# Channel mixer, hidden pairs f = 3 to 9: two plain products replaced by Strassen's seven, with weight sums made by GpSimd

## The chip, the core and the metric

The kernel runs on one core of one Trainium2 chip. The metric is the device time of one execution in microseconds (us); lower is better. Engines are named as in the profile: PE is TensorE (matmuls), PEld its weight loads, DVE is VectorE, ACT is ScalarE, POOL is GpSimd, SP is SyncE. SPq and POOLq are the DMA issues of SP and POOL. Each engine takes its instructions strictly in the order of its own list; that list is fixed when the kernel is built.

## The reference, cut to what matters

One layer: two token mixers, then a SwiGLU channel mixer with 22 hidden blocks of 128 channels, then a norm.

```python
h2 = rmsnorm(x, norm2_w[l])                                   # 512 tokens x 1024
f_gate, f_up = jnp.split(h2 @ ffn_w_gate_up[l], 2, axis=-1)   # 2816 + 2816 columns
x = x + (jax.nn.silu(f_gate) * f_up) @ ffn_w_down[l]
return rmsnorm(x, norm_f_w)
```

Each fp32 product is made of three matmuls: both factors are split into a rounded part ("hi") and the rest ("lo"), and hi·hi, hi·lo and lo·hi are added.

## The kernel before, in words

The change lies in the first half of the channel mixer, from about 618 to 843 us of the profiled execution. A **pair** f (0 to 21) is hidden block f of the gate (`wgu[f]`) and of the up projection (`wgu[FF + f]`), over all 512 tokens.

**Plain pairs, f < F0 = 10** (lines 1076 to 1098). `col_tile` calls `unit`, which loads a 128x1024 weight tile `raw` by SP, lets ACT write `whi` (L111) and DVE the rest `wlo` (L112), and issues 24 matmuls of 512 columns (8 blocks of the inner dimension, three terms each). A pair is two such tiles: 48 matmuls. ACT makes the silu `cw` (L1086), DVE the product `fm`. The pairs f = 0 and 1 are partly done ahead, in `norm2`.

**Strassen pairs, f >= F0** (`pair`, from L1109). The gate and up tiles, each cut in two halves of the inner dimension, are the blocks A11, A12, A21, A22 of a 2x2 matrix; the activations are cut in four likewise. Seven products of 12 matmuls each, 256 columns wide, take the place of the 48 wide ones: 84 matmuls. They need four weight units, in this order: `w` = (A11, A12), `w46` = (A22, s2), `w37` = (s4, s3), `w5` = (s1), with s1 = A21 + A22, s2 = A11 + s1, s3 = A11 + A21, s4 = A12 + s2. These sums are read from DRAM.

**Who makes the sums.** `feed_one` (L186) has SP copy one block within DRAM and then has POOL issue a DMA that adds the other block to it (L196). This goes on from the first stage of the kernel to about 736 us, one sum per weight unit. An s2 waits for its s1, an s4 for its s2.

**The sums for the down projection.** `dsums_to(f)` does, for odd f and while any are left, one round of this: POOL issues a load of a 1 MB tile `wst` (L166), adds blocks in it by four 128x512 additions (L172), and issues the store to `wsum` (L173). The pool of `wst` has one buffer, so that the next load waits until the store has left it. Four rounds are left for this stage.

**The activations' sums** `xb0` to `xb3` and their splits T1 to T4 (`th`, `tl`) are made by DVE and ACT from a list `todo`, one entry per weight tile, spread over the plain pairs. `some_operands(f)` makes the operands `fh`, `fl` of the down projection from the finished `fm`, from f = 7 on.

**Buffers and order.** `raw`, `whi` and `wlo` have three buffers each: ACT can write the `whi` of a unit when PE has finished the unit three places before. The order in which each engine gets its instructions is not that of the code: a scheduler at build time places them by dependences, priorities and its own estimates. So an instruction written late can stand early in its engine's list.

Of the kernel before, what the change touches and what calls it, by code (L numbers as in the profile page):

```python
# [14 lines left out]
P = 128  # L15
T = 512
# [4 lines left out]
FF = 22  # L21
# [11 lines left out]
def block_kernel(ctx, tc, a):  # L33
    nc = tc.nc
    V, S, G, PE = nc.vector, nc.scalar, nc.gpsimd, nc.tensor
# [3 lines left out]
    wp = ctx.enter_context(tc.tile_pool(name="wp", bufs=3))  # L39
# [57 lines left out]
    loads, start_feed, gps_ = [], [False], []  # L97
# [3 lines left out]
    def unit(ap, pool=None):  # L101

        aps = ap if isinstance(ap, tuple) else (ap,)
        n = T * len(aps) if isinstance(ap, tuple) else 1024
        raw, hi, lo = ((pool or wp).tile([P, n if pool else 1024], t, name=x)[:, 0:n]
                       for t, x in ((F32, "raw"), (F32R, "whi"), (F32R, "wlo")))
        for i, p in enumerate(aps):
            loads.append(nc.sync.dma_start(raw[:, i * T:(i + 1) * T] if len(aps) > 1 else raw, p))
        if start_feed[0]:
            fill()  # L110
        marked(S.activation(hi, raw, AF.Copy), "unit")  # L111
        marked(V.tensor_tensor(out=lo, in0=raw, in1=hi.bitcast(F32), op=ALU.subtract), "unit")  # L112
        return hi, lo
# [31 lines left out]

    FK, F0 = FF // 2, 10
    sums = {n: dram.tile([FF - F0, P, T], F32, name=n, bufs=1) for n in ("s1", "s2", "s3", "s4")}
    gu = {n: a["wgu"][r * FF + F0:(r + 1) * FF][:, :, c * T:(c + 1) * T]  # L150
          for n, r, c in (("A11", 0, 0), ("A12", 0, 1), ("A21", 1, 0), ("A22", 1, 1))}
# [13 lines left out]
    def dsums_load(k, r, eng, cs=slice(0, T)):  # L165
        eng.dma_start(r, a["wdn"][k].rearrange("p (i c) -> p i c", i=4)[:, :, cs])  # L166
# [33 lines left out]
    def fill():  # L200

        units[0] += 1
        if units[0] % 3 != 2 or not gps_:
            feed_one()
        if taken and units[0] % 3 != 2 and not norming[0]:
            dsums_add(*taken.pop(0))
        if halves and gps_ and units[0] > 3 and not taken and not norming[0] and (units[0] % 2 == 0 if len(gps_) == 1 else units[0] % 3 == 0):
            half_load()
# [3 lines left out]
    with tc.tile_pool(name="st", bufs=2) as st:  # L212
# [56 lines left out]
        for k in range(KD):  # L269
            w = vec[:, k:k + 1]  # L270
# [3 lines left out]
            if k % 2 == 0:  # L274
                c = slice(k * P, k * P + 256)
# [24 lines left out]
        raw, hi, lo = early[3]  # L300
# [41 lines left out]
        for k in range(2, 4):  # L342
# [6 lines left out]
                        in1=ss[:, 1].rearrange("p (n a) -> p n a", a=1).broadcast_to([P, NT, 16]), op=ALU.mult)  # L349
# [6 lines left out]
                        in1=rowp[:, 1:2, :].broadcast_to([P, NT, H]), op=ALU.add)  # L356
# [9 lines left out]
        with tc.issue_after(ln_.ins):  # L366
            for g_ in gated:
# [8 lines left out]
                        op=ALU.mult)  # L376
# [445 lines left out]
    while step() or chains:  # L822
# [4 lines left out]
        for c in list(chains):  # L827
            if c[0] <= count[0] or not queue:
                with behind():
                    n = next(c[1], None)  # L830
# [160 lines left out]
    fxs = ctx.enter_context(ExitStack())  # L991
# [9 lines left out]
    def tt(out, in0, in1, op, eng=V):  # L1001
        return eng.tensor_tensor(out=out, in0=in0, in1=in1, op=op)  # L1002
# [5 lines left out]
    def hidden():  # L1008
        fms.append(fp.tile([P, T], F32, name="fm"))
        return fms[-1]  # L1010
# [17 lines left out]
    def dsums_to(f):  # L1028
        if f % 2 and rest:
            k, cs = rest.pop(0)  # L1030
            if rest and rest[0][0] == k:
                rest.pop(0)
                cs = slice(0, T)
            r = fs.tile([P, 4, T], F32, name="wst")[:, :, 0:cs.stop - cs.start]
            dsums_load(k, r, nc.gpsimd, cs)
            dsums_add(k, r, cs)
# [25 lines left out]
    def some_operands(f):  # L1062
        if not ff:
            fxs.close()
            ff.append(ctx.enter_context(tc.tile_pool(name="ff", bufs=FK)))
        for _ in range(3 if f < F0 else 2):
            if len(made) <= f:
                operands(len(made))
                made.append(1)

    def next_todo():
        if todo:
            with behind():
                todo.pop(0)()

    for f in range(F0):
        start_feed[0] = f > 0
        dsums_to(f)
        if f > 1:
            pg = psm.tile([P, T], F32, name="mm")  # L1080
            col_tile(pg, a["wgu"][f], hhk, hlk)
        else:
            pg = first[2 * f][0]
            k_loop(*first[2 * f], slice(2 * P, T))
        sg = fq.tile([P, T], F32, name="cw", bufs=2)
        S.activation(sg, pg, AF.Silu)  # L1086
        if f:
            next_todo()
            pu = psm.tile([P, T], F32, name="mm")
            col_tile(pu, a["wgu"][FF + f], hhk, hlk)  # L1090
        else:
            pu = first[1][0]
            k_loop(*first[1], slice(2 * P, T))
        tt(hidden(), pu, sg, ALU.mult)
        if f:
            next_todo()
        if f > 6:
            some_operands(f)

    def hprod(ps, w, i, x):  # L1100

# [7 lines left out]
    def pair(f):  # L1109

        z = [bank() for _ in range(4)] if f % 2 == 0 else [bank(), bank2(), bank2(), bank2()]
        s = lambda n: sums[n][f - F0]
        w = unit(a["wgu"][f])
        w46 = unit((a["wgu"][FF + f][:, T:], s("s2")))
        hprod(z[0][:, t1], w, 0, B11)
        hprod(z[1][:, t1], w, 1, B21)
        hprod(z[2][:, t1], w46, 0, T4)
        w37 = unit((s("s4"), s("s3")))
        hprod(z[0][:, t2], w46, 1, T2)
        cw = fq.tile([P, T], F32, name="cw", bufs=2)  # L1120
        S.copy(out=cw[:, t1], in_=z[0][:, t1])
        u = fq.tile([P, TH], F32, name="cu")
        tt(u, cw[:, t1], z[0][:, t2], ALU.add)
        hprod(z[1][:, t2], w37, 0, B22)
        w5 = unit((s("s1"),))
        hprod(z[3][:, t1], w37, 1, T3)
        v = fq.tile([P, TH], F32, name="cv2")
        tt(v, u, z[3][:, t1], ALU.add)
        if f == F0:
            xsplit(*T1, b11)  # L1130
        hprod(z[2][:, t2], w5, 0, T1)
        tt(cw[:, t2], u, z[2][:, t2], ALU.add)
        fm = hidden()
        tt(fm.rearrange("p (i t) -> p i t", i=2), z[2].rearrange("p (i t) -> p i t", i=2),
           v.rearrange("p (a t) -> p a t", a=1).broadcast_to([P, 2, TH]), ALU.add)
        tt(cw, cw, z[1], ALU.add)
        S.activation(cw, cw, AF.Silu)
        V.scalar_tensor_tensor(out=fm, in0=fm, scalar=-1.0, in1=cw, op0=ALU.mult, op1=ALU.mult)

    for f in range(F0, FF):  # L1140
        pair(f)
        dsums_to(f)
        some_operands(f)


    fqs.close()
# [220 lines left out]
```

## Time and profile before

| | us |
|---|---|
| median of 3 runs (lowest to highest) | 957.11 (956.86 to 957.43) |
| the profiled execution | 957.3 |
| its span | 955.5 |
| outside the span | 1.8 |
| first matmul of f = 2 | 634.29 |
| first matmul of f = 10 (first Strassen pair) | 721.33 |
| first matmul of the down projection | 842.82 |
| POOL busy, whole span | 350.4 |

Views used: the page's busy times and its chain; the waits of an engine in a stretch of time; the timeline of one engine, where a row is start, busy time, engine, line, operation, output<-inputs, how many such instructions in a row (then the busy time is that of all), and in brackets the idle time before it and what ended it. PE rows overlap, since matmuls are pipelined: their pace is read from start to start, not from the busy time.

### The profile page before, as it was taken

Reading aid. Unit: us, or ns where it says so; the run is one execution under the profiler, and the core shown is the slowest. Engines: PE = TensorE matmul, PEld = TensorE weight load, DVE = VectorE, ACT = ScalarE, POOL = GpSimd, SP = SyncE. Lnnn points to the kernel's source line nnn. Section 1 sums busy time; section 2 is a strip of 40 time slices with the busy share of each in tenths; the row PEclk is TensorE's granted clock in tenths of the full one; section 3 lists DMA queues with packets and bytes.
Section 4 is the critical chain, followed back from the end, with each engine's and each line's share of the span. In section 5 each row is a group of like instructions: output and inputs, shape, how many; then the busy total and the mean of one; then the engine's idle time right before and its main releaser. Section 6 shows DMA issues by size and latency. Waiting matters only on the chain.

```text
span 955.5 us, 14889 instructions
## 1 busy us (share of the span) xinstructions
PE 942.1 (99%) x5208; PEld 794.2 (83%) x5208; DVE 729.6 (76%) x1134; ACT 535.3 (56%) x1102; POOL 350.4 (37%) x555
## 2 busy tenths in 40 slices
PE   9999999999999999999999999999999999999997
PEld 6778888887887888888877888888889999988885
DVE  4999887876888888898877753766425887888896
ACT  7697786969756674634546323323324445456545
POOL 1136434344533447444163432254351111133042
PEclk9999999999999999999999999999999999999999
DMA  9234322233232246979887984598899655578654
GB/s 324 104 128 118 102 82 86 92 99 101 70 92 87 89 133 158 316 223 267 273 274 220 315 235 172 181 264 290 277 255 216 198 188 190 177 228 262 210 178 155
DMA packets 78186, 177.39 MB, mean 186 GB/s; under 512 B 10080, under 2 KB 19472, under 8 KB 77088
## 3 DMA queue, kind: packets, MB, share of 16 engines
q1 hardware_dynamic: 66528, 144.89, 45.5%
q0 software_dynamic: 10288, 28.90, 13.4%
q10 hardware_dynamic: 1296, 2.67, 0.7%
q8 instruction: 41, 0.67, 0.3%
q14 instruction: 33, 0.27, 0.1%
HBM read 156.22 MB, written 45.37 MB: 211 GB/s over the span
## 4 chain that ended last, share of the span: by engine, by line
PE 85%; ACT 3%; DVE 3%; issue 2%; DMA 1%; POOL 1%; POOLq 0%; SPq 0%; ACTq 0%; DVEq 0%
PE mm L121 57%; PE w L121 19%; PE g L437 1%; DMA raw<-s 1%; DVE wlo L112 1%; PE st L616 1%; PE st L610 1%; PE b L542 1%; PE g L470 1%; PE b L548 1%; PE b L566 1%; PE st L604 1%; PE g L519 1%; PE st L615 1%; PE st L605 1%
## 5 line engine op out<-in xcount | busy, mean ns | idle before, releaser
L111 ACT ACTIVATE whi<-raw 128x1024 fp32r<-128x1024 f32 (+1 forms) x191 | 196.2, 1029 | 240.7 <-PE mm L121 143.6
L112 DVE TENSOR_TENSOR wlo<-raw,whi 128x1024 fp32r<-128x1024 f32 (+1 forms) x191 | 240.5, 1260 | 88.0 <-ACT whi L111 87.4
L121 PE MATMUL mm<-hh,whi 128*128 128x512 f32 (+1 forms) x688 | 268.9, 391 | 0.3 <-ACT hh L336 0.3
L121 PE MATMUL mm<-hl,whi 128*128 128x512 f32 (+1 forms) x688 | 264.4, 384 | 0.0
L121 PE MATMUL mm<-hh,wlo 128*128 128x512 f32 (+1 forms) x688 | 263.6, 384 | 0.2 <-DVE wlo L112 0.2
L672 DVE SCALAR_TENSOR_TENSOR cps<-c,c31w,cps 128x512 f32<-128x512 f32 x240 | 180.3, 751 | 6.1 <-ACT cps L670 1.8
L121 PEld LDWEIGHTS mm<-hh,wlo 128*128 128x128 f32 x688 | 129.6, 188 | 23.6 <-DVE wlo L112 0.4
L121 PEld LDWEIGHTS mm<-hh,whi 128*128 128x128 f32 x688 | 129.7, 189 | 22.5 <-ACT hh L336 0.8
L121 PEld LDWEIGHTS mm<-hl,whi 128*128 128x128 f32 x688 | 129.9, 189 | 20.8
L1002 POOL TENSOR_TENSOR fm<-fm 128x256 f32<-128x256 f32 x33 | 28.0, 850 | 111.9 <-DVE s L1002 87.4
L424 DVE SCALAR_TENSOR_TENSOR acc<-mm,c4w,acc 128x511 f32<-128x511 f32 (+2 forms) x72 | 53.1, 741 | 6.1 <-ACT acc L421 5.9
L506 POOL TENSOR_TENSOR ytm<-U,y 128x60 f32<-128x60 f32 (+14 forms) x120 | 37.1, 309 | 48.2 <-DMA U<-sc 39.4
L121 PE MATMUL mm<-yl,whi 128*128 128x512 f32 x128 | 50.0, 391 | 2.3 <-DVE yl L861 2.3
L121 PE MATMUL mm<-yh,whi 128*128 128x512 f32 x128 | 50.7, 396 | 0.0
L121 PE MATMUL mm<-yh,wlo 128*128 128x512 f32 x128 | 49.9, 390 | 0.0
L121 PE MATMUL w<-hh,wlo 128*128 128x256 f32 x168 | 47.7, 284 | 0.3 <-DVE wlo L112 0.3
L121 PE MATMUL w<-hh,whi 128*128 128x256 f32 x168 | 47.6, 284 | 0.0
L121 PE MATMUL w<-hl,whi 128*128 128x256 f32 x168 | 47.5, 283 | 0.0
L121 PE MATMUL w<-wlo,fh 128*128 128x512 f32 (+1 forms) x115 | 44.3, 385 | 0.2 <-DVE wlo L112 0.2
L121 PE MATMUL w<-whi,fh 128*128 128x512 f32 (+1 forms) x115 | 44.2, 385 | 0.0
L121 PE MATMUL w<-whi,fl 128*128 128x512 f32 (+1 forms) x115 | 44.2, 384 | 0.0
L196 POOL DMA_DIRECT2D s<-in_wgu_dram x24 | 23.6, 997 | 47.9 <-DMA s<-in_wgu_dram 47.9
(332 smaller groups left out, 1915.8 us busy)
## 6 DMA issues: line engine op xcount, KB each, us to landing
raw<-in_win_dram SPq DMA_DIRECT2D x61, 512.0 KB, 3.5
raw<-in_wgu_dram SPq DMA_DIRECT2D x32, 512.0 KB, 3.6
s<-in_wgu_dram SPq DMA_DIRECT2D x48, 256.0 KB, 5.3
raw<-s SPq DMA_DIRECT2D x48, 256.0 KB, 3.6
raw<-wsum SPq DMA_DIRECT2D x44, 256.0 KB, 3.8
raw<-in_wdn_dram SPq DMA_DIRECT2D x33, 256.0 KB, 3.5
s<-in_wgu_dram POOLq DMA_DIRECT2D x24, 256.0 KB, 7.2
s<-s POOLq DMA_DIRECT2D x24, 256.0 KB, 7.0
```

The costliest lines, as they stand in the source:

```text
L111: marked(S.activation(hi, raw, AF.Copy), "unit")
L112: marked(V.tensor_tensor(out=lo, in0=raw, in1=hi.bitcast(F32), op=ALU.subtract), "unit")
L121: marked(PE.matmul(ps, l, r, start=first and i == 0, stop=last and i == 2))
L196: fed.append(nc.gpsimd.dma_start(*begun.pop(0), accum_op=ALU.add, max_dma_last_dim=2048))
L424: marked(V.scalar_tensor_tensor(out=acc[:, s:], in0=ps[:, :T - s], scalar=c4w[:, j, k:k + 1], in1=acc[:, s:], op0=ALU.mult, op1=ALU.add))
L437: PE.transpose(ps[:, n, :], src[:, n, :], ident)
L470: PE.matmul(ps[:, n, :], kT[:, n, :], kT[:, n, :], start=True, stop=True)
L506: G.tensor_tensor(out=tm[:, :, 0:w], in0=U[:, k, :, k + 1:], in1=y[:, :, k:k + 1].broadcast_to([P, NT, w]), op=ALU.mult)
L519: PE.matmul(ps[:, n, :], kT[:, n, :], qT[:, n, :], start=True, stop=True)
L542: PE.matmul(ps[:, n, 0:16], Ud[:, n, :], xc[:, n, 0:16], start=True, stop=True)
L672: V.scalar_tensor_tensor(out=acc, in0=c[:, k:k + T], scalar=c31w[:, i, k:k + 1], in1=acc, op0=ALU.mult, op1=ALU.add)
L1002: return eng.tensor_tensor(out=out, in0=in0, in1=in1, op=op)
```

## The change

Pairs f = 3 to 9 go through `pair` too (FS = 3). Their weight sums are not taken from DRAM. `summed(f)` loads the gate and the up tile of pair f into one tile `z` of seven 128x512 blocks (two buffers) and has POOL add four times within it: s3 = A11 + A21, then s1 in the place of A21, then s2, then s4. It is called for f = 3 during f = 0, and otherwise at the start of the pair before. `halves_of` takes the place of `unit` and splits blocks of `z`: no `raw` tile is loaded.

The loop of plain pairs is left with f = 0, 1, 2. Their `next_todo` takes three entries at a time instead of one. `dsums_to` and `some_operands` are called from f = 10 on only; `some_operands` then makes up to two operands a call.

```diff
-    FK, F0 = FF // 2, 10
+    FK, FS, F0 = FF // 2, 3, 10
...
-        for _ in range(3 if f < F0 else 2):
+        for _ in range(2):
...
+    fz = fxs.enter_context(tc.tile_pool(name="fz", bufs=2))
+    zs = {}
+    def summed(f):
+        z = zs[f] = fz.tile([P, 7, T], F32, name="z")
+        for i, r in ((0, f), (2, FF + f)):
+            loads.append(nc.sync.dma_start(z[:, i:i + 2].rearrange("p i c -> p (i c)"), a["wgu"][r]))
+        a11, a12, a21, a22, s2, s4, s3 = (z[:, i] for i in range(7))
+        for o, x, y in ((s3, a11, a21), (a21, a21, a22), (s2, a11, a21), (s4, a12, s2)):
+            tt(o, x, y, ALU.add, G)
+    def halves_of(z, i, n=2):
+        hi, lo = (wp.tile([P, 1024], F32R, name=x)[:, 0:n * T] for x in ("whi", "wlo"))
+        if start_feed[0] and i in (0, 5):
+            fill()
+        src = z[:, i:i + n].rearrange("p i c -> p (i c)")
+        marked(S.activation(hi, src, AF.Copy), "unit")
+        marked(V.tensor_tensor(out=lo, in0=src, in1=hi.bitcast(F32), op=ALU.subtract), "unit")
+        return hi, lo
...
-    for f in range(F0):
+    for f in range(FS):
         start_feed[0] = f > 0
-        dsums_to(f)
...
-        if f > 6:
-            some_operands(f)
+        else:
+            summed(FS)
...
-        w = unit(a["wgu"][f])
-        w46 = unit((a["wgu"][FF + f][:, T:], s("s2")))
+        if f + 1 < F0:
+            summed(f + 1)
+        w = halves_of(zs[f], 0) if f < F0 else unit(a["wgu"][f])
+        w46 = halves_of(zs[f], 3) if f < F0 else unit((a["wgu"][FF + f][:, T:], s("s2")))
...
-    for f in range(F0, FF):
+    for f in range(FS, FF):
         pair(f)
-        dsums_to(f)
-        some_operands(f)
+        if f >= F0:
+            dsums_to(f)
+            some_operands(f)
```

**POOL's list.** Before the change, in the plain pairs, the rounds of `wst` (one number for each round) alternate with the issues of the feed (L196):

```order
L172 TENSOR_TENSOR wst_6452<-wst_6452 128x512 x4
L173 DMA wsum_136<-wst_6452 128x2048
L196 DMA s3_127<-in_wgu_dram 128x512
L166 DMA wst_6594<-in_wdn_dram 128x2048
L196 DMA s2_126<-s1_125 128x512
L196 DMA s1_125<-in_wgu_dram 128x512
L172 TENSOR_TENSOR wst_6594<-wst_6594 128x512 x4
```

After the change, from the last addition but one for f = 4 (tile `z_6611`) to the third for f = 5 (tile `z_6740`):

```order
L1002 TENSOR_TENSOR z_6611<-z_6611 128x512
L166 DMA wst_8043<-in_wdn_dram 128x2048
L1002 TENSOR_TENSOR z_6611<-z_6611 128x512
L172 TENSOR_TENSOR wst_8043<-wst_8043 128x512 x4
L173 DMA wsum_137<-wst_8043 128x2048
L166 DMA wst_8318<-in_wdn_dram 128x2048
L172 TENSOR_TENSOR wst_8318<-wst_8318 128x512 x4
L173 DMA wsum_138<-wst_8318 128x2048
L1002 TENSOR_TENSOR z_6740<-z_6740 128x512
L196 DMA s1_125<-in_wgu_dram 128x512
L1002 TENSOR_TENSOR z_6740<-z_6740 128x512
L196 DMA s4_128<-s2_126 128x512
```

All four rounds of `wst`, called from f = 11 on in the code, stand among the additions for f = 3 to 6; two whole rounds stand between those for f = 4 and those for f = 5. Right behind, the last round stands around the first additions for f = 6 (tile `z_6867`):

```order
L1002 TENSOR_TENSOR z_6740<-z_6740 128x512
L166 DMA wst_8599<-in_wdn_dram 128x2048
L1002 TENSOR_TENSOR z_6740<-z_6740 128x512
L172 TENSOR_TENSOR wst_8599<-wst_8599 128x512 x3
L1002 TENSOR_TENSOR z_6867<-z_6867 128x512
L172 TENSOR_TENSOR wst_8599<-wst_8599 128x512
L1002 TENSOR_TENSOR z_6867<-z_6867 128x512
L196 DMA s3_127<-in_wgu_dram 128x512
L1002 TENSOR_TENSOR z_6867<-z_6867 128x512
```

The third addition of each `z` is s2, which `w46` needs; the first round (`wst_7768`) is mixed likewise with the four additions for f = 3 (`z_6455`). For f = 7 to 9 no round is left among them.

**DVE's list.** DVE now has the activations' sums and splits close together, ahead of the first `wlo` taken from `z`; before, each stood between two weight tiles. After the change, from the `wlo` of the gate of f = 2:

```order
L112 TENSOR_TENSOR wlo_6532<-raw_6530,whi_6531 128x1024
L1002 TENSOR_TENSOR xb2_6392<-xb2_6392,xb0_6390 128x1024
L1002 TENSOR_TENSOR xb3_6393<-hh_92,hl_93 128x1024
L112 TENSOR_TENSOR wlo_6571<-raw_6569,whi_6570 128x1024
L1002 TENSOR_TENSOR xb3_6393<-xb2_6392,xb3_6393 128x1024
L1051 SCALAR_TENSOR_TENSOR tl0_6395<-xb2_6392,th0_6394 128x1024
L1002 TENSOR_TENSOR fm_6524<-mm_6491,cw_6486 128x512
L999 TENSOR_TENSOR tl2_6399<-xb3_6393,th2_6398 128x1024
L999 TENSOR_TENSOR tl1_6397<-xb1_6391,th1_6396 128x1024
L1090 TENSOR_TENSOR wlo_6619<-z_6455,whi_6618 128x1024
```

The work on the activations that stood between the weight tiles of f = 1 to 9 now stands before the first product of f = 3.

More of the change, by code (lines that the diff above doesn't have):

```diff
@@ L1069, in some_operands @@
                 made.append(1)
-    def next_todo():
-        if todo:
-            with behind():
-                todo.pop(0)()
-    for f in range(F0):
+    fz = fxs.enter_context(tc.tile_pool(name="fz", bufs=2))
[15 more added lines that the diff above has]
+        return hi, lo
+    def next_todo():
+        for _ in range(3):
+            if todo:
+                with behind():
+                    todo.pop(0)()
+    for f in range(FS):
         start_feed[0] = f > 0
-        dsums_to(f)
         if f > 1:
@@ L1117, in pair @@
         hprod(z[2][:, t1], w46, 0, T4)
-        w37 = unit((s("s4"), s("s3")))
+        w37 = halves_of(zs[f], 5) if f < F0 else unit((s("s4"), s("s3")))
         hprod(z[0][:, t2], w46, 1, T2)
@@ L1124, in pair @@
         hprod(z[1][:, t2], w37, 0, B22)
-        w5 = unit((s("s1"),))
+        w5 = halves_of(zs[f], 2, 1) if f < F0 else unit((s("s1"),))
         hprod(z[3][:, t1], w37, 1, T3)
@@ L1128, in pair @@
         tt(v, u, z[3][:, t1], ALU.add)
-        if f == F0:
+        if f == FS:
             xsplit(*T1, b11)
```

## The prediction

> **What bounds the kernel now.** First the page's busy times and its chain, then what PE waited for between 600 and 845 us (a row is engine, line, waited for, total, times, longest).
>
> ```profile
> span 955.5 us, 14889 instructions
> PE 942.1 (99%) x5208; PEld 794.2 (83%) x5208; DVE 729.6 (76%) x1134; ACT 535.3 (56%) x1102; POOL 350.4 (37%) x555
> PE 85%; ACT 3%; DVE 3%; issue 2%; DMA 1%; POOL 1%; POOLq 0%; SPq 0%; ACTq 0%; DVEq 0%
> PE w L121 <- DVE wlo L112: 0.3, 1, 0.3
> PE mm L121 <- DVE wlo L112: 0.2, 1, 0.2
> ```
>
> PE is busy for 99% of the span, carries 85% of the chain, and in the stage of the change waits 0.5 us in all. The number of matmuls times their pace sets the time here, so fewer columns help; and any wait that PE gets is added to the end in full. The pace comes from three first matmuls on PE's timeline:
>
> ```profile
> 634.29 0.39 PE L121 MATMUL mm<-hh,whi 128*128 128x512 f32 x1
> 721.33 0.28 PE L121 MATMUL w<-hh,whi 128*128 128x256 f32 x1
> 842.82 0.40 PE L121 MATMUL w<-whi,fh 128*128 128x512 f32 x1
> ```
>
> They begin f = 2, f = 10 and the down projection. Eight plain pairs take 721.33 - 634.29 = 87.04 us, 10.88 each; twelve Strassen pairs 121.49 us, 10.12 each, or 0.1205 for each of 84 matmuls.
>
> **What the change removes.** Seven pairs at 10.88 - 10.12 = 0.76 us: **5.3 us off PE**, if it never waits. All else is whether the operands come in time.
>
> **What it adds.** POOL gets 28 additions of 128x512. The same shape stands in the rounds of `wst` (L172); POOL's timeline has all four rounds:
>
> ```profile
> 618.17 0.87 POOL L166 DMA_DIRECT2D wst<-in_wdn_dram  x1
> 625.29 0.81 POOL L196 DMA_DIRECT2D s<-s  x1 [5.12 <-DMA s<-s]
> 627.68 8.55 POOL L172 TENSOR_TENSOR wst<-wst 128x512 f32<-128x512 f32 x4 [1.58 <-DMA wst<-in_wdn_dram]
> 636.53 0.60 POOL L173 DMA_DIRECT2D wsum<-wst  x1 [0.30 <-POOL wst L172]
> 642.86 0.57 POOL L166 DMA_DIRECT2D wst<-in_wdn_dram  x1 [4.86 <-issue]
> 651.11 7.13 POOL L172 TENSOR_TENSOR wst<-wst 128x512 f32<-128x512 f32 x4 [5.97 <-DMA wst<-in_wdn_dram]
> 658.54 0.59 POOL L173 DMA_DIRECT2D wsum<-wst  x1 [0.30 <-POOL wst L172]
> 664.02 0.57 POOL L166 DMA_DIRECT2D wst<-in_wdn_dram  x1 [4.02 <-DMA wsum<-wst]
> 664.58 0.89 POOL L196 DMA_DIRECT2D s<-in_wgu_dram  x1
> 674.13 5.78 POOL L172 TENSOR_TENSOR wst<-wst 128x512 f32<-128x512 f32 x4 [8.67 <-DMA wst<-in_wdn_dram]
> 680.22 0.59 POOL L173 DMA_DIRECT2D wsum<-wst  x1 [0.31 <-POOL wst L172]
> 685.71 0.56 POOL L166 DMA_DIRECT2D wst<-in_wdn_dram  x1 [4.03 <-DMA wsum<-wst]
> 693.90 6.46 POOL L172 TENSOR_TENSOR wst<-wst 128x512 f32<-128x512 f32 x4 [6.75 <-DMA wst<-in_wdn_dram]
> ```
>
> Read from it: an addition costs 1.44 us (5.78 / 4) to 2.14 (8.55 / 4), 1.75 in the mean of the four (6.98 / 4). From the issue of a load to the first addition pass 9.5, 8.3, 10.1 and 8.2 us, 9.0 in the mean. From the issue of a store to the next load 6.3, 5.5 and 5.5, mean 5.8. An issue takes 0.6 (wst) or about 0.85 (feed). Before, a wait on POOL delayed only other sums needed far later.
>
> Why 8.55 in one round and 5.78 in another is seen on DVE's timeline:
>
> ```profile
> 627.16 1.22 DVE L112 TENSOR_TENSOR wlo<-raw,whi 128x1024 fp32r<-128x1024 f32 x1
> 628.29 2.32 DVE L1002 TENSOR_TENSOR xb<-xb,xb 128x1024 f32<-128x1024 f32 x1
> 630.54 2.31 DVE L112 TENSOR_TENSOR wlo<-raw,whi 128x1024 fp32r<-128x1024 f32 x1
> 635.00 0.68 DVE L1002 TENSOR_TENSOR fm<-mm,cw 128x512 f32<-128x512 f32 x1
> 637.24 1.21 DVE L1002 TENSOR_TENSOR xb<-xb,xb 128x1024 f32<-128x1024 f32 x1
> ```
>
> POOL adds from 627.68 to 636.23. Well inside, a DVE operation with both inputs in SBUF takes 2.32 (2.25 from start to start); after it 1.21. One that reads PSUM (`mm`) takes its usual 0.68. So the two engines slow each other: 2.14 on POOL and 2.25 on DVE while both work in SBUF.
>
> **The step that decides** is POOL's list. Two whole rounds of `wst` stand between the last addition for f = 4 and the first for f = 5, and one load of `wst` before the first for f = 6. POOL takes its list in order: at 674.13 it had stood idle for 8.67 us for its load. Step by step, with 0.3 from an addition's end to the store:
>
> - Round 1 and f = 3: eight additions from 627.68 at 2.14 (DVE works throughout: ten operations of 2.25 wait for it), an s4 issue and a store: 627.68 + 17.1 + 0.8 + 0.6 = 646.2.
> - f = 4: three additions and two feed issues ahead of the load of round 2: + 6.4 + 1.7 = 654.3.
> - Round 2: + 9.0 to the first addition, + 7.0 for four, + 0.3 + 5.8 to the next load: 676.4.
> - Round 3: + 9.0, + 5.8 for four (DVE stands by then), + 0.9 for the store: 692.1.
> - f = 5: three additions at 1.44 and two feed issues: + 6.0 = 698.1. Then ACT's `whi`, 1.06 in the row below, and DVE's `wlo`, 1.2: PE can go on at **700.4**.
>
> ```profile
> 639.70 1.06 ACT L111 ACTIVATE whi<-raw 128x1024 fp32r<-128x1024 f32 x1 [4.38 <-PE mm L121]
> ```
>
> PE would want this `wlo` in f = 5's third product: 634.29 + 10.88 + 2 x 10.12 + 24 x 0.1205 + 0.24 = 668.5. **It waits 31.9 us.** Nothing on ACT or DVE can pass: the `whi` and `wlo` that wait are ahead of all that is for later pairs.
>
> - f = 6: the load of round 4 is issued behind the third addition, at 698.1; + 9.0, then seven additions to this pair's s2 (three of `wst`, `z`, `wst`, `z`, `z`) at 1.6, between alone and contended since DVE is half idle, and one feed issue: 719.2; + 2.3 = **721.5**. PE wants it at 700.1 + 60 x 0.1205 + 2.89 + 0.24 = 710.5: **11.0 more.**
> - The rest of f = 6 is 60 matmuls: 721.2 + 7.2 = 728.5. Then the clock:
>
> ```profile
> 1.00 4.02 PE L258 MATMUL g<-one 128*128 128x512 bf16 x9 [1.00 <-DVE epsc L73]
> 7.10 0.39 PE L121 MATMUL mm<-ul,whi 128*128 128x512 f32 x1
> 7.33 0.40 PE L121 MATMUL mm<-uh,whi 128*128 128x512 f32 x1
> 948.00:950.00 2.00, 0.36 (x4) 0.16 (x2) 1.55 (x7) 0.18 (x2) 0.17 (x1) 1.00 0.68 262
> 952.00:954.00 2.00, 0.00 (x0) 0.00 (x0) 0.00 (x0) 0.00 (x0) 0.00 (x0) 0.59 0.59 229
> 954.00:955.50 1.50, 0.00 (x0) 0.00 (x0) 0.00 (x0) 0.00 (x0) 0.00 (x0) 0.50 0.00 0
> ```
>
> At the start nine matmuls take 0.45 each, and a start-to-start of 0.23 comes only from 7.10: about 5.9 us at half pace. At the end (stretches; PE busy first, granted clock last but two) PE stops at 948.4 and the clock is halved by about 952.4. Waits of 32 and 11 us halve it too. The first slow stretch lies in front of a wait for POOL and costs nothing; the second costs at most 5.9 / 2 = 2.9, nothing at least; I take 2.9: 731.4. The Trainium skill's page "TensorE: Matmul & The Clock Gate" (Part 1, What's actually happening) puts the warm-up at about 3.4 us; by it the cost would be 1.7, an estimate, and the sum 1.2 less.
>
> - f = 7 to 9: POOL needs 4 x 1.44 to 4 x 2.14 plus two issues, 7.5 to 10.3, against 10.12 for PE, and starts with 2.6 us in hand; no wait. 3 x 10.12 = 30.4: f = 10 starts at 761.8.
>
> Before, it started at 721.33: **40.5 later**, the 5.3 saved included. The profiled execution took 957.3 (0.2 above the median, 1.8 beyond its span): 997.8, or **997.6** beside the median.
>
> **Edits at no cost.** SP loads two `z` halves instead of two `raw` tiles, as many bytes, past the feed's copies; a buffer of `z` comes free a pair ahead, which hides the 4.7 us that such a load takes here (row below). If `z` lands late for f = 3, up to 3 us more at the head of POOL's chain. The feed keeps two sums per pair, and its last sums are for pairs ten places on. The `todo` list moved together makes DVE late for f = 3: from 627.16 ten operations at 2.25 and one of 0.6 end at 650.3, where PE wants the last at 645.4. This wait of 4.9 us is hidden: POOL's chain does not wait for PE, so PE only arrives at f = 5 later. Ten operands moved behind f = 9 are 10 x 0.35 = 3.5 us of DVE (five took 1.77, row below) within two pairs of 10; wholly uncovered they cost that, and I take 0, since PE reaches each `wlo` some 3 us after its buffer came free.
>
> ```profile
> 670.89 1.77 DVE L999 TENSOR_TENSOR fl<-fm,fh 128x256 fp32r<-128x256 f32 x5 [0.48 <-ACT fh L998]
> raw<-in_wgu_dram SPq DMA_DIRECT2D x18, 512.0 KB, 4.7
> ```
>
> **Rivals.**
> - *POOL's rounds do not hold up the additions* (faster). Without the two rounds, s2 for f = 5 is there by 654.3 + 2.1 + 8.1 = 664.5, before 666.2, so the case turns on the rounds taking under 2 us; the rows give some 20 each. It needs POOL to pass a waiting instruction. Then 957.3 - 5.3 = 952.0. Chance 0.07.
> - *Only DVE is late*: the rounds are hidden, the 4.9 us at f = 3 are not: 956.9, no change. Chance 0.04.
> - *Loads are faster while PE stands.* The store of the same 1 MB lands in 5.2:
>
> ```profile
> wst<-in_wdn_dram POOLq DMA_DIRECT2D x4, 1024.0 KB, 8.8
> wsum<-wst POOLq DMA_DIRECT2D x3, 1024.0 KB, 5.2
> ```
>
>   With 5.4 instead of 9.0 in the three loads of the chain, 10.8 less: 987. For it: few other transfers then; against: no load took under 8.2. Chance 0.13. The Trainium skill, "DMA: Bandwidth & Descriptors" (Anatomy of one DMA), has 2.0 us plus bytes / 436e3 for such a DMA, 4.4 for 1 MB (an estimate); the trace's 8.2 to 10.1 differ, and by it the sum would be 984.
> - *Worse*: additions contended throughout (seven taken at 1.44, seven at 1.6 and four at 1.75 all at 2.14: + 10.3) and loads of 10.1 (+ 3.3): 1011. Chance 0.12.
> - The forecast: 0.64.
>
> **Numbers.** All terms at their low ends (no contention 10, loads and stores 3, clock 2.9) give 982, at their high ends (the worse rival's 13.6 and a late `z`) 1014. These ends do not come together; 984 to 1009 leaves out the first two rivals (0.11) and the tail of the worse one. About 0.2% is what a measurement of this kernel can tell from no change. Slower: 0.64 + 0.13 + 0.12 = 0.89; no change 0.04; faster 0.07.
>
> **What would show it.** POOL idle twice for `wst` between its additions for f = 4 and f = 5, and once before f = 6; PE waiting about 32 us in f = 5 and 11 in f = 6 for `wlo`, with ACT's `whi` behind POOL's `z`; the granted clock halved there; 10.12 per pair in f = 7 to 9 and all later stages unchanged in length. Wrong, if POOL's additions for f = 5 come before those of `wst`, or PE's waits lie elsewhere.

## The result, and the profile after

| | us | f=10 starts | down projection starts |
|---|---|---|---|
| before, median of 4 runs | 956.99 (956.07 to 957.43) | 721.33 | 842.82 |
| after, median of 4 runs | 990.94 (988.83 to 993.84) | 754.01 | 875.38 |

The ratio is 1.0366, 95% interval 1.0347 to 1.0385: the change makes the kernel slower by 34 us. The profiled execution after took 989.89 us. The starts are those of the profiled executions. In each of the runs 3, 7 and 9 below one execution took 1148 to 2375 us, far from all the others of its kernel; their medians, ranges and ratios leave it out (with it, run 9's median would be 958.74).

The page's busy times and the chain's shares by engine after, beside which stand the waits of PE from 600 to 900 us:

```profile
span 988.1 us, 15508 instructions
PE 945.0 (96%) x5460; PEld 808.1 (82%) x5460; DVE 777.2 (79%) x1183; ACT 548.9 (56%) x1123; POOL 391.6 (40%) x583
PE 71%; DVE 6%; DMA 6%; POOL 6%; ACT 4%; issue 3%; POOLq 0%; SPq 0%; DVEq 0%; ACTq 0%
```

```profile
PE mm L121 <- ACT whi L1089: 18.6, 1, 18.6
PE w L121 <- ACT whi L1089: 5.0, 1, 5.0
PE w L121 <- DVE wlo L1090: 4.9, 2, 3.1
PE mm L121 <- DVE wlo L1090: 1.0, 1, 1.0
PE w L121 <- DVE wlo L112: 0.3, 1, 0.3
PE mm L121 <- DVE wlo L112: 0.2, 1, 0.2
```

PE was busy for 99% of the span and carried 85% of the chain; now it is 96% and 71%. In this stage it waited 0.5 us and now waits 30. Nearly all of that is for `whi` and `wlo` made from `z` (L1089, L1090).

Where the waits lie is read from PE's starts. A pair is 84 matmuls; counted back from the first matmul of the down projection (`w<-whi,fh`), every 84th begins a pair. Three of these rows, the first matmuls of f=3, f=5 and f=6, and the one of f=10:

```profile
646.74 0.28 PE L121 MATMUL w<-hh,whi 128*128 128x256 f32 x1
670.50 0.28 PE L121 MATMUL w<-hh,whi 128*128 128x256 f32 x1
702.79 0.29 PE L121 MATMUL w<-hh,whi 128*128 128x256 f32 x1
754.01 0.28 PE L121 MATMUL w<-hh,whi 128*128 128x256 f32 x1
```

| pair | 3 | 4 | 5 | 6 | 7 | 8 | 9 | 10 | 11 | 12 on |
|---|---|---|---|---|---|---|---|---|---|---|
| us | 13.68 | 10.08 | 32.29 | 20.63 | 10.08 | 10.08 | 10.43 | 10.08 | 10.49 | 10.08 |

An undisturbed pair takes 10.08 (the 10.12 before held f=11's 10.56). So f=5 has 22.2 us too many and f=6 10.6; f=3 has 3.6. The sum closes: seven pairs took 107.27 where plain ones took 7 x 10.88 = 76.16, 31.1 more; the stage began 1.6 later than before; together 32.7, against 988.1 - 955.5 = 32.6 for the spans. The 1.6 are not shown to be the change's. Near 520 us, in a stage that the change does not touch, PE waits for VectorE in both traces (2.3 us before, 2.1 after); behind it the granted clock (last but two) was full before and lower after, which is worth 5 x 0.34 = 1.7 us (first before, then after):

```profile
520.00:525.00 5.00, 5.00 (x21) 3.81 (x22) 5.00 (x9) 0.57 (x1) 0.00 (x0) 1.00 1.00 270
```

```profile
520.00:525.00 5.00, 4.75 (x14) 3.77 (x15) 5.00 (x10) 1.09 (x2) 0.27 (x1) 0.66 0.98 276
```

POOL's timeline shows what f=5 and f=6 waited for:

```profile
654.49 0.59 POOL L166 DMA_DIRECT2D wst<-in_wdn_dram  x1
655.09 1.69 POOL L1002 TENSOR_TENSOR z<-z 128x512 f32<-128x512 f32 x1
660.07 7.15 POOL L172 TENSOR_TENSOR wst<-wst 128x512 f32<-128x512 f32 x4 [3.29 <-DMA wst<-in_wdn_dram]
667.52 0.58 POOL L173 DMA_DIRECT2D wsum<-wst  x1 [0.30 <-POOL wst L172]
672.97 0.54 POOL L166 DMA_DIRECT2D wst<-in_wdn_dram  x1 [4.87 <-DMA wsum<-wst]
679.37 5.27 POOL L172 TENSOR_TENSOR wst<-wst 128x512 f32<-128x512 f32 x4 [5.86 <-DMA wst<-in_wdn_dram]
684.94 0.55 POOL L173 DMA_DIRECT2D wsum<-wst  x1 [0.30 <-POOL wst L172]
685.50 1.27 POOL L1002 TENSOR_TENSOR z<-z 128x512 f32<-128x512 f32 x1
...
690.29 1.18 POOL L166 DMA_DIRECT2D wst<-in_wdn_dram  x1
691.04 1.73 POOL L1002 TENSOR_TENSOR z<-z 128x512 f32<-128x512 f32 x1
699.02 4.89 POOL L172 TENSOR_TENSOR wst<-wst 128x512 f32<-128x512 f32 x3 [6.25 <-DMA wst<-in_wdn_dram]
```

The last addition for f=4 ends at 656.8; the first for f=5 starts at 685.50. The 28.7 us between them are two rounds of `wst`: 12.4 of additions, 14.6 of idling ahead of additions, stores and loads, the rest issues. ACT's rows carry the wait on, one in f=5 and one in f=6:

```profile
690.99 1.06 ACT L1089 ACTIVATE whi<-z 128x1024 fp32r<-128x1024 f32 x1 [23.37 <-POOL z L1002]
...
709.68 1.06 ACT L1089 ACTIVATE whi<-z 128x1024 fp32r<-128x1024 f32 x1 [9.76 <-POOL z L1002]
```

The stretches of PE's two long waits (PE busy first, granted clock last but two):

```profile
668.00:700.00 32.00, 12.42 (x84) 11.92 (x83) 8.21 (x12) 4.58 (x6) 14.47 (x15) 0.68 0.64 207
712.00:722.00 10.00, 7.35 (x47) 7.35 (x48) 10.00 (x8) 3.27 (x5) 8.01 (x7) 0.67 0.73 175
```

After each wait the matmuls of 256 columns start 0.21 us apart at first, in place of 0.12; that is 2.6 us of f=5's 22.2 (19.6 are waits) and 2.5 of f=6's 10.6 (8.0 are waits). The same happens in f=3 after a far shorter wait: PE waited 1.9 us for `wlo`, and 1.5 us later, from 650.5 to 653.7, the matmuls start 0.21 apart (the granted clock is 0.57 over 650 to 654). So nearly half of f=3's 3.6 us is the clock, and a short wait can cost about twice its length.

### The profile page after: what moved, and what is told of

It reads as the page before. It is cut to its first block, busy times and chain, and to the rows that moved or that the text cites. A ratio compares the mean times of both kernels' runs of the same rounds, so it can differ in the third digit from the quotient of the medians.

```text
span 988.1 us, 15508 instructions
## 1 busy us (share of the span) xinstructions
PE 945.0 (96%) x5460; PEld 808.1 (82%) x5460; DVE 777.2 (79%) x1183; ACT 548.9 (56%) x1123; POOL 391.6 (40%) x583
## 4 chain that ended last, share of the span: by engine, by line
PE 71%; DVE 6%; DMA 6%; POOL 6%; ACT 4%; issue 3%; POOLq 0%; SPq 0%; DVEq 0%; ACTq 0%
PE mm L121 44%; PE w L121 18%; DMA wst<-in_wdn_dram 3%; POOL wst L172 2%; POOL z L1002 2%; DVE wlo L1090 2%; DVE wlo L112 1%; PE g L437 1%; DMA gsl<-sgd 1%; PE b L542 1%; PE st L616 1%; PE g L470 1%; PE b L548 1%; PE st L610 1%; PE b L566 1%
## 5 line engine op out<-in xcount | busy, mean ns | idle before, releaser
L112 DVE TENSOR_TENSOR wlo<-raw,whi 128x1024 fp32r<-128x1024 f32 (+1 forms) x177 | 219.9, 1244 | 62.1 <-ACT whi L111 61.9
L121 PE MATMUL mm<-hh,whi 128*128 128x512 f32 (+1 forms) x624 | 239.3, 384 | 0.3 <-ACT hh L336 0.3
L121 PE MATMUL mm<-hl,whi 128*128 128x512 f32 (+1 forms) x624 | 235.0, 377 | 0.0
L121 PE MATMUL mm<-hh,wlo 128*128 128x512 f32 (+1 forms) x624 | 234.0, 376 | 0.0
L1090 DVE TENSOR_TENSOR wlo<-z,whi 128x1024 fp32r<-128x1024 f32 (+1 forms) x28 | 46.4, 1677 | 32.8 <-ACT whi L1089 32.8
L121 PE MATMUL w<-hh,wlo 128*128 128x256 f32 x232 | 66.1, 285 | 2.3 <-DVE wlo L1090 1.9
L121 PE MATMUL w<-hh,whi 128*128 128x256 f32 x232 | 65.7, 284 | 0.0
L1089 ACT ACTIVATE whi<-z 128x1024 fp32r<-128x1024 f32 (+1 forms) x28 | 26.6, 949 | 63.1 <-POOL z L1002 44.2
L1002 POOL TENSOR_TENSOR z<-z 128x512 f32<-128x512 f32 x28 | 48.9, 1746 | 9.9 <-DMA z<-in_wgu_dram 9.6
L121 PE MATMUL w<-th,whi 128*128 128x256 f32 x148 | 43.4, 293 | 5.0 <-ACT whi L1089 5.0
```

The costliest lines, as they stand in the source:

```text
L121: marked(PE.matmul(ps, l, r, start=first and i == 0, stop=last and i == 2))
L1089: marked(S.activation(hi, src, AF.Copy), "unit")
L1090: marked(V.tensor_tensor(out=lo, in0=src, in1=hi.bitcast(F32), op=ALU.subtract), "unit")
```

## The experiments

Each ratio is to runs of the kernel before on the same chip, whose medians were 955.75 to 956.99. Pair times and waits are those of one execution, the profiled one.

| run | sums on POOL | rounds of `wst` | us | ratio, 95% interval |
|---|---|---|---|---|
| changed kernel | yes | among the additions | 990.94 | 1.0347 to 1.0385 |
| two rounds late | yes | two there, two late | 972.48 | 1.0154 to 1.0184 |
| rounds late | yes | behind the additions | 970.48 | 1.0113 to 1.0155 |
| rounds behind the feed | yes | behind additions and feed | 970.38 | 1.0122 to 1.0183 |
| late, no rounds | yes | none | 957.35 | 0.9993 to 1.0036 |
| no sums | no | in the stage | 956.56 | 0.9985 to 1.0015 |
| no sums, no rounds | no | none | 950.59 | 0.9930 to 0.9962 |

**1. The rounds behind the additions.** The edit, in the changed kernel (`zlast[0]` is the last addition given out so far):

```diff
-            dsums_load(k, r, nc.gpsimd, cs)
-            dsums_add(k, r, cs)
+            with tc.issue_after(zlast[0].ins):
+                dsums_load(k, r, nc.gpsimd, cs)
+                dsums_add(k, r, cs)
```

> The change with all four rounds of wst placed behind the last z addition (f = 9) in POOL's list; nothing else differs. Theory 'POOL's list' (the rounds' DMA waits stand ahead of the additions): no wait in f = 5 and f = 6, and with four instead of eight additions on POOL before f = 3 DVE is in time there too; seven pairs at Strassen pace leave 957.0 - 5.3 = 951.7 us, within 1.5. Rival 'the additions themselves' (28 additions on POOL and the mutual slowing with DVE are what PE waits for): these stay and only 16 of 44 go, so about a third of the 34 us of waits goes: about 980. Rival 'DVE late at f = 3': the waits in f = 5 and 6 go, some 4 us at f = 3 stay: about 956.

Measured: 970.48 (967.91 to 976.53). Pairs f=5 and f=6 take 10.08 each: their waits are gone, so it was POOL's list that made them. But the time falls to 970, not 952. PE's waits, 640 to 800 us, show what is left:

```profile
PE w L121 <- ACT whi L111: 4.6, 4, 2.3
PE mm L121 <- DVE wlo L1091: 2.7, 2, 1.6
PE w L121 <- DVE wlo L112: 2.4, 4, 0.8
PE w L121 <- DVE wlo L1091: 1.9, 1, 1.9
```

f=3 takes 13.69, f=7 13.31 (waits for `wlo`, L1091), and f=10 to f=16, now beside the rounds, 15.6 too many in all, 5.1 in f=12 and 5.4 in f=13. So there are further costs, which the changed kernel's long waits had covered: in f=3 and f=7, and beside the rounds wherever they stand. The profiled execution, 976.53, is the slowest of the five. With two smaller rows (1.0 and 0.8) the waits make 13.4 of the 22.4 us that its pairs have too many. Much of the rest is the clock again, granted at 0.66 over each of 651 to 656, 753 to 758 and 767 to 772 us, 1.7 us each.

**2. Two of the rounds there, two late.** The same edit for the third and fourth round alone (`if len(rest) < 4`).

> The change with rounds 3 and 4 of wst behind the last z addition, rounds 1 and 2 where the change has them. 'POOL's list': POOL goes from the store of round 2 (667.5 in the changed kernel) straight to f = 5, whose s2 is split by about 675.5, where PE wants it at about 673.7: a wait of about 2 us in f = 5 instead of 22, none in f = 6; the 3.6 us at f = 3 stay. 957.0 - 5.3 + 3.6 + 2 = 957, from 955 to 960. 'The additions themselves': half of the rounds' additions gone, about 974.

Measured: 972.48 (972.08 to 973.13). The time lies near the 974 of the rival and far from the 957 of the theory, but its place is not the rival's: f=6 takes 10.08, and f=5 19.27, 9.2 too many, where two rounds ahead of it cost 22.2. Of these 9.2, 2.8 are the wait for the sum that was forecast at about 2; PE then waits 2.5 for a slow `wlo`, and the clock is granted at 0.53 from 672 to 683 us. One round in front of a needed sum is enough for a wait. The rest lies in f=3 (12.07), f=7 (12.47) and f=10 to f=13 (7.5 too many in all).

**3. No additions, the rounds in the stage.**

```diff
-        for o, x, y in ((s3, a11, a21), (a21, a21, a22), (s2, a11, a21), (s4, a12, s2)):
-            tt(o, x, y, ALU.add, G)
...
+        i = {0: 0, 3: 2, 5: 0, 2: 2}[i]
         src = z[:, i:i + n].rearrange("p i c -> p (i c)")
```

> The change without the 28 z additions: the units of f = 3 to 9 are taken from the loaded blocks where sums would stand. Rounds of wst stay in the stage. 'POOL's list' and 'the additions themselves' both say: PE waits for POOL nowhere, 951.7, up to 1.5 more if DVE is late at f = 3 while round 1 adds. If the seven-product pairs cost something by themselves (their loads, splits, PSUM), it shows here: above 954.

The products take loaded blocks where sums would stand. Measured: 956.56 (952.46 to 957.90). f=3 to f=9 take 10.08 each: seven products cost nothing but their matmuls, and 5.6 us are saved by f=10 (7 x (10.88 - 10.08)). All of it goes in one pair: f=11 takes 16.34. ACT's row in f=11, and POOL's list ahead of it:

```profile
728.91 1.06 ACT L111 ACTIVATE whi<-raw 128x1024 fp32r<-128x1024 f32 x1 [6.38 <-DMA raw<-s]
```

```profile
691.33 7.29 POOL L172 TENSOR_TENSOR wst<-wst 128x512 f32<-128x512 f32 x4 [6.37 <-DMA wst<-in_wdn_dram]
698.92 0.60 POOL L173 DMA_DIRECT2D wsum<-wst  x1 [0.30 <-POOL wst L172]
699.51 0.89 POOL L196 DMA_DIRECT2D s<-in_wgu_dram  x1
700.09 1.14 POOL L196 DMA_DIRECT2D s<-s  x1
700.62 1.44 POOL L196 DMA_DIRECT2D s<-in_wgu_dram  x1
```

The sums of f=11 come from DRAM, and POOL issues the DMAs that make them. Three such issues follow at once on the round that kept POOL from 685 to 699. Of f=11's 6.3 us PE waits 3.1 (2.4 for `whi`, 0.7 for `wlo`); most of the rest is the clock, granted at 0.57 from 730 to 738 us. In the kernel before, f=11 took 10.56.

**4. The kernel before with 56 additions more** (eight of 128x256, as much as four of 128x512, in each pair f=3 to f=9; nobody reads them).

```diff
+        if f > 2:
+            for i in range(8):
+                extra = fq.tile([P, TH], F32, name="extra")
+                x = fms[f - 1][:, i % 2 * TH:i % 2 * TH + TH]
+                tt(extra, x, x, ALU.add, G)
```

> The kernel before with as much GpSimd addition as the change brings, 8 of 128x256 for each pair from f = 3 to 9, whose results nothing reads. 'POOL's list': POOL and DVE slow each other but PE waits for neither: 957.0, within 1. 'The additions themselves': the mutual slowing alone makes PE wait: 962 or more.

Measured: 956.54 (955.20 to 959.44), ratio 0.9992 to 1.0017, no change. They ran later than the code says, among and behind the rounds in POOL's list: 31 beside plain pairs, from 665.9 us on, and 25 beside f=10 to f=12, up to 748. So plain pairs have the slack for them, at the least from f=5 on.

**5. Neither additions nor rounds.** Run 3 with `dsums_to` emptied, and the plain `wdn` in place of the sums not made.

> As the run without additions, and the four wst rounds are left out too (the down projection reads the plain wdn tiles in their place, so neither sum is made). In the run without additions f=3 to f=9 ran at 10.08 us each, and f=11 took 16.34, 6.26 too many, with a wait for raw, loaded from the DRAM sums s. Theory: the DMA accumulates that make these sums stand in POOL's list behind the adds of the last round (699.5, right after that round's store at 698.9). Then f=11 runs at 10.08 without rounds, and the time is 956.6 - 6.3 = 950.3 us (949.5 to 951.5). Rival: the sums' own chain, copies by SP and then one accumulate after another of some 8 us each, sets the pace; then f=11 still waits 4 us or more, and the time stays at 955 to 957.

Measured: 950.59 (950.48 to 951.60). Every pair from f=3 to f=21 takes 10.08. This is what the change has to give at most: 6.2 us by the two medians, 5.6 from the pairs and 0.5 from f=11's old wait. And f=11's wait in run 3 goes with the rounds.

**6. All additions, no rounds.** Run 1 with `dsums_to` emptied in the same way.

> All GpSimd additions as in the changed kernel, none of the four wst rounds (the down projection reads the plain wdn tiles in their place, so four of the wdn sums are left out). The run with the rounds behind the additions took 970.5, with 3.6 us too many in f=3, 3.2 in f=7 and some 16 in f=10 to f=16. Theory: the 16 us come from the rounds (their adds beside Strassen pairs, and the accumulates of the feed behind them); then f=10 to f=16 run at 10.08 to 10.3, f=3 and f=7 stay, and the time is 951 + 3.6 + 3.2 = 957.8 us (956 to 960). Rival: the additions themselves delay the feed of f=10 to f=13, since the accumulates stand between them in POOL's list; then f=11 to f=13 still lose 6 to 10 us and the time is 963 to 968.

Measured: 957.35 (953.61 to 964.91). So the additions alone cost 957.35 - 950.59 = 6.8 us, as much as the change saves, and the rounds behind them the other 13 of run 1 (970.48 - 957.35, on two chips whose kernels before differ by 1.0). The profiled execution, 964.91, was the slowest of its ten; beside f=3 (13.69) and f=7 (13.15) it has 5.1 too many in f=9 to f=11, which the forecast didn't have. The median is what f=3 and f=7 alone would give (950.59 + 3.6 + 3.1 = 957.3), but no trace of a median execution shows that.

**7. Run 3 with a faster feed.** One condition taken from `fill`. It held only while the stages ahead of the channel mixer ran, so the feed is ahead when the mixer begins.

```diff
-        if units[0] % 3 != 2 or not gps_:
-            feed_one()
+        feed_one()
```

> As the run without additions, rounds kept, and the feed gives out one copy at every fill, not at two of three, so that the sums for f=10 on are begun earlier. If the feed's own pace made f=11 wait, the wait of 6.3 us goes and the time is 950.3 us (949.5 to 952). If the accumulates are late because they stand behind the rounds' adds in POOL's list, an earlier copy helps by only a part: f=11 keeps 2 us or more and the time is 953 to 957.

Measured: 953.31 (950.96 to 955.37), ratio 0.9945 to 0.9975. f=11 takes 10.08 with the rounds in place: for f=11 an earlier feed serves as well as no rounds. Yet the time is 2.7 above run 5's. f=3 starts at 646.96 against 643.95 in run 3, and PE's one wait for `sacc`, ahead of the mixer, is 2.5 us in place of 0.2. That the feed costs this is not shown. In the traces without the faster feed f=3 starts anywhere from 643.45 to 647.52 us, and those have a wait of PE near 520 (up to 2.9 us) that this one lacks. What takes the 2.7 us stays open.

**8. The rounds behind additions and feed.** Run 1's edit with `fed[-1]`, the last accumulate, for `zlast[0]`, and `if f > F0 + 1 and f % 2 and rest` in `dsums_to`.

> The whole computation: the four wst rounds are given out in f=13, 15, 17 and 19, behind the feed's last accumulate in POOL's list, so that neither the additions nor the feed stand behind a round. If the feed behind the rounds cost f=10 to f=13 their some 12 us in the run with late rounds, these go and only some 1 us in each of four to six pairs beside a round is left, with f=3 (3.6) and f=7 (3.2): 951 + 6.8 + 5 = 962.8 us (959 to 965). If it was the rounds' adds and transfers beside Strassen pairs that cost them, the loss moves with the rounds to f=14 to f=20, and the time stays at 967 to 973.

Measured: 970.38 (967.68 to 972.69). f=10 to f=13 keep 2.7 of the 12.5 that they lost in run 1, but f=14 to f=18 now lose 9.2 (f=16 3.5, with a clock of 0.66 over 789 to 794). PE's waits from 640 to 850:

```profile
PE w L121 <- DVE wlo L1091: 4.7, 4, 1.9
PE w L121 <- DVE wlo L112: 4.7, 5, 1.7
PE w L121 <- ACT whi L111: 1.2, 2, 1.0
PE mm L121 <- DVE wlo L112: 1.2, 2, 0.8
```

10.6 of the 11.8 us of waits are for VectorE's `wlo`, and the time is run 1's: the loss moved with the rounds, as the second forecast has it. The first of them was added from 740.5 on, in f=11 and f=12, so that some of the 2.7 is theirs too: a round beside Strassen pairs costs 2.3 to 3 us here (9.2 / 4 to 11.9 / 4), and 3.9 in run 1's trace (15.6 / 4).

**9 and 10. Sums that nobody waits for.** Run 6 with the additions writing only blocks that no product reads.

```diff
-        for o, x, y in ((s3, a11, a21), (a21, a21, a22), (s2, a11, a21), (s4, a12, s2)):
+        for o, x, y in ((s3, a11, a21), (s2, a21, a22), (s4, a11, a21), (s4, a12, s2)):
...
+        i = {0: 0, 3: 2, 5: 0, 2: 2}[i]
```

> All 28 additions run on GpSimd as in the run with late additions and no rounds (957.35), with the same operands and size, but no product reads what they write: the products take the loaded blocks in place of the sums, and no rounds are made, so those sums are missing from the output. Pairs f=3 and f=7 lost 3.6 and 3.1 us there. Theory: GpSimd's adds slow VectorE's operations that stand beside them (a 128x1024 subtraction 2.31 us in place of 1.21), and VectorE's lo halves come late; then f=3 and f=7 lose as much when nobody waits for a sum, and the time is 957 us (955.5 to 959). Rival: the sums come too late for the products; then these waits go and the time is that without additions and rounds, 950.6 us (950 to 952.5).

> The kernel with unread sums once more, for a trace: the profiled run of the first time ran at 0.555 of the clock (1545.9 us), and its pairs can't be read. Theory (VectorE slowed by GpSimd's adds): f=3 takes 13.2 to 14 us and f=7 12.5 to 13.5, both with waits for lo halves from VectorE, though no product waits for a sum; the time is 955.5 to 960 us. Rival (sums late): both take 10.08 us, and the 958.7 of the first time came from elsewhere.

Measured: 957.63 (955.39 to 963.50) and, the second time, 958.17 (955.06 to 961.36); without additions it was 950.59. So the additions cost 7 us or more though no product waits for a sum, and the rival's 950 to 952.5 is out. The trace is of the second. PE's waits from 640 to 850 are one row, two waits:

```profile
PE w L121 <- DVE wlo L1086: 5.1, 2, 3.8
```

f=3 takes 11.63, f=6 15.64, f=9 10.48, all else 10.08: 7.5 too many. The pairs are not those foreseen: f=3 loses 1.6 in place of 3 to 4, f=7 nothing. The cause is the one foreseen, VectorE's `wlo` beside additions; but 5.5 of the 7.5 hang on a single operation, in f=6:

```profile
674.97 7.32 DVE L1086 TENSOR_TENSOR wlo<-z,whi 128x1024 fp32r<-128x1024 f32 x1 [0.55 <-ACT whi L1085]
```

While it ran POOL made five additions and three DMA issues with hardly a pause. Its 7.3 us are about what it takes alone (1.22) and five additions take alone (1.2 to 1.3 each) together, as if it had stood for all five; what happens inside it the trace does not show. PE waited 3.8 us for it, and the clock behind it (0.66 over 683 to 688) took 1.7 more. Two groups of the same operation, VectorE's `wlo` of 128x1024 from `z` between 640 and 715 us (count, busy, mean ns, idle time before), with unread sums and, in run 5, without:

```profile
L1086 DVE TENSOR_TENSOR wlo<-z,whi 128x1024 fp32r<-128x1024 f32 x21 | 36.7, 1752 | 7.3 <-ACT whi L1085 7.2
```

```profile
L1083 DVE TENSOR_TENSOR wlo<-z,whi 128x1024 fp32r<-128x1024 f32 x20 | 24.5, 1223 | 18.6 <-ACT whi L1082 18.6
```

The same operation takes 1752 ns in the mean in place of 1223 (some 1470 without the long one), and the idle time before it falls from 18.6 us to 7.3: VectorE has less slack, and some `wlo` come late.

That f=7 loses nothing here bears on runs 1 and 6, where it lost 3.2 and 3.1. Its rows in run 1, first ACT's and then VectorE's:

```profile
691.86 1.06 ACT L1090 ACTIVATE whi<-z 128x1024 fp32r<-128x1024 f32 x1 [3.28 <-POOL z L1002]
692.95 3.27 DVE L1091 TENSOR_TENSOR wlo<-z,whi 128x1024 fp32r<-128x1024 f32 x1 [1.42 <-ACT whi L1090]
```

ACT stood for a sum that came late, and then the subtraction took 3.27 us: ahead of f=7's first wait stand both a late sum and a slowed VectorE. f=3's wait is for its first `wlo`, which needs no sum. How run 6's 6.8 us divide between the two is not shown; unread sums show that the slowing alone can cost as much.

**11. The kernel before with eight unread additions in each of the pairs f=12 to f=21.** The edit of run 4, in `pair`, for `f > F0 + 1`.

> The kernel before, with eight GpSimd additions of 128x256 that nobody reads in each of the ten pairs f=12 to f=21 (these pairs ran at 10.08 us; 28 adds more beside plain pairs cost nothing). Eight take some 7.6 us of GpSimd (955 ns each in the run with 28), against 6.7 for a pair's four adds of 128x512. VectorE is busy 7.1 to 7.9 us of a 10.08 us pair. If additions beside such a pair cost it time through VectorE, each pair grows by 0.5 to 1 us and the time is 956.7 + 5 to 10 = 962 to 967 us. If they cost nothing but where the sums are awaited, 956.7 us (956 to 958).

Measured: 960.99 (959.75 to 961.43), ratio 1.0040 to 1.0071: between the two forecasts. f=12 to f=15 take 10.08, f=16 to f=21 10.73 each. PE waits eight times, always for VectorE, six of them in these six pairs and two in the down projection; `wlo` takes 1575 ns between 780 and 844 us, and 1224 in the kernel before:

```profile
PE w L121 <- DVE wlo L112: 2.9, 8, 0.4
```

```profile
L112 DVE TENSOR_TENSOR wlo<-raw,whi 128x1024 fp32r<-128x1024 f32 x19 | 29.9, 1575 | 3.7 <-ACT whi L111 3.7
```

So the price exists outside the changed pairs too, where no sum is awaited. Two stretches, f=13 to f=15 and f=17 to f=20 (PE busy first, DVE third, POOL fifth):

```profile
749.30:779.50 30.20, 30.20 (x254) 30.20 (x253) 26.96 (x34) 14.37 (x21) 26.94 (x29) 1.00 0.57 180
790.30:833.20 42.90, 41.31 (x338) 40.50 (x337) 38.45 (x49) 19.52 (x29) 38.55 (x41) 1.00 0.56 170
```

VectorE and POOL are both busy for 0.89 to 0.90 of either, yet only the second has waits. Why they begin at f=16 is not settled.

**12. Only f=8 and f=9 through seven products.** `FS = 8`, the additions given out in f=4 and f=5, so that they run beside plain pairs, `dsums_to` in the plain pairs as before but behind `zlast[0]`, and run 7's feed. The whole computation is kept.

> The whole computation: only pairs f=8 and f=9 go through seven products, their eight additions are made in the plain pairs ahead, GpSimd's list has them before rounds 2 to 4, and the feed gives a copy at every fill. By the runs so far: additions beside plain pairs cost nothing, each pair saves 0.8 us (10.88 to 10.08), f=11's wait of 0.48 us goes: 956.7 - 1.6 - 0.5 = 954.6 us (953 to 956.5, the upper end if the faster feed takes back up to 2 us ahead of the stage, as it may have in the run with it). If the additions or the rounds that they push back make a new wait, 958 to 963 us.

Measured: 957.36 (955.44 to 958.96), ratio 1.0001 to 1.0021; the forecast of 953 to 956.5 is missed. Every pair from f=8 on takes 10.08, as forecast. Part of the saving is spent ahead of them: f=8 starts at 700.30, where before it was at 721.33 - 2 x 10.88 = 699.57; PE's wait for `sacc` stands at 1.3 us. In the profiled executions (956.3 against 957.3) 1 us of the forecast 2.1 is left; the medians (957.36 against 956.11) have nothing of it, and what takes it there is not settled. No version tried beats the kernel before with the whole computation.

## Why the prediction was right, step by step

The prediction was 997.6, range 984 to 1009; the time is 990.94. The mechanism was the forecast's; the terms were not all its size, and some errors cancelled.

- **PE bounds, 5.3 us saved.** Right: 7 x (10.88 - 10.08) = 5.6. Run 3 has all of it by f=10.
- **POOL's list decides.** Right, and shown by run 1, where moving the rounds alone brings f=5 and f=6 to 10.08. Point by point against the steps: round 2's load issued at 654.49 (predicted 654.3, by luck, as the next point has it); the next load at 672.97 (676.4); f=5's first addition at 685.50 (692.1); the additions for s2 done and the fourth load issued at 690.29 (698.1).
- **Two errors cancel before round 2.** Round 1's load took 10.8 us, so that POOL's first addition came 2.9 later than the predicted 627.68; f=4's three additions and two issues took 6.1 in place of 8.1, and round 1 with f=3 0.6 less than predicted.

```profile
619.76 0.86 POOL L166 DMA_DIRECT2D wst<-in_wdn_dram  x1
630.54 3.94 POOL L172 TENSOR_TENSOR wst<-wst 128x512 f32<-128x512 f32 x2 [8.96 <-DMA wst<-in_wdn_dram]
```

- **The term that was off is the load of `wst`.** It was taken as 9.0 from issue to first addition. The three loads of the chain took 5.6, 6.4 and 8.7. The first two make 6.0 of the 7.8 us by which 690.29 is earlier; f=5's additions (4.8 in place of 6.0) make most of the rest. This is the rival "loads are faster while PE stands" in part, and not by its reason: the 5.6 us load ran from 654.49, while PE still worked without a pause, and the 8.7 us one while PE stood for only 2.8 us of it. Nothing here tells which transfers slow them.
- **The wait of f=5.** Predicted 31.9, measured 18.6 + 1.0. PE has its `wlo` at 693.92 in place of 700.4, which takes off 6.5, and came to the wait 5.2 later, at 673.5 in place of 668.3, since the stage began 1.6 late and f=3 lost 3.6. That shortens the wait and not the time.
- **f=3's late VectorE, 4.9 us, hidden.** Right in the changed kernel: its 3.6 us, 1.9 of waiting and the rest the clock, which the prediction did not have there, only let PE come to f=5's wait later. But the cover was the rounds' own, and run 1, which takes it away, shows the 3.6 in full.
- **f=6.** Predicted 11.0, measured 8.0. The sum was there at 709.7, 9.5 before the predicted 719.2: the 7.8 carried over, and seven additions that took 10.2 us instead of 11.2. In return `wlo` took 3.83 us in place of 1.2, so PE went on with it at 714.65, predicted 721.5:

```profile
710.77 3.83 DVE L1090 TENSOR_TENSOR wlo<-z,whi 128x1024 fp32r<-128x1024 f32 x1 [8.52 <-ACT whi L1089]
```

- **The clock.** 2.9 were taken behind f=6's wait and none behind f=5's. Both are there, 2.6 and 2.5, and the first costs nothing for the reason given, since f=6's additions end on POOL's time.
- **f=7 to f=9 without a wait.** Right but for 0.35 in f=9. f=10 starts at 754.01, predicted 761.8: again 7.8 us earlier. That it is the same figure as ahead of f=6 is luck, since within f=6 the lead was 9.5 at the sum and 6.9 at its `wlo`.
- **The feed at no cost, since "its last sums are for pairs ten places on".** True of this kernel (f=11 took 10.49, before 10.56), whose f=11 begins 33 us later than before. Without that delay the feed takes back the whole saving (run 3 against run 5). The step's reason was wrong.
- **The rival of POOL passing its rounds, 952.0.** Its time was wrong even for its own case: with the rounds out of the way the additions still cost 6.8 us (run 6), and the rounds some 13 in both of the places they were moved to (runs 1 and 8). The prediction had the slowing of both engines as a term of POOL's chain and of f=3, and not as a cost of later pairs.

## What to carry to other kernels

Where an engine takes its list in order, look at what a new addition stands behind, in the list of the built kernel and not in the code: two background transfers there cost this kernel more than the whole change could give. A saving on the bounding engine moves its deadlines forward for everyone else, so take the work that was "needed far later" and subtract the saving from its slack. And work given to an idle engine is not free when it slows the one beside it: before the change, compare the second engine's slack in a pair with what the slowing takes, and count a wait of 2 to 3 us of PE at up to twice its length, for the clock behind it.

## What the runs showed of the hardware

- VectorE and GpSimd, both working in SBUF, slow each other: a 128x1024 subtraction takes 1.22 us alone, 2.3 beside additions, 2.5 to 3.3 where two or three additions or DMA issues of GpSimd follow each other, and in one place each 3.83 (changed kernel) and 7.32 (run 10); an addition of 128x512 takes 1.2 to 1.3 alone and up to 2.28 beside VectorE.
- The lower clock after waits of 18.6 and 1.0 us and after waits of 5.0 and 3.1 us cost about the same, 2.6 and 2.5 us, and after one of 1.9 us 1.7.
- After waits of 2 to 3 us it does not always come: after 2.1 us near 520 in the changed kernel it did, after 2.3 at the same place in the kernel before it did not; after f=3's 1.9 us it did in the changed kernel and in runs 1 and 6, and did not in run 8.
- The four loads of the same 1 MB took 10.8, 5.6, 6.4 and 8.7 us within 80 us of one execution, with no order by the bytes moved over them in all: 348, 298, 346 and 168 GB/s.
